# A chunked-scan decay mask built by TensorE in PSUM instead of by broadcast loads, in a hybrid encoder block on one core

## The chip, the cores and the metric

The kernel runs on one core of a Trainium2 chip, in float32. The metric is the device time of one execution in microseconds (us), as the median of several runs; smaller is better.

## The reference

The block takes x (1024 tokens by 1024) and computes h = RMSNorm(x), one combined projection, two mixers side by side, an output projection with a residual, and a squared-ReLU MLP. The first mixer is a Mamba-2 scan that runs over the tokens in both directions, in chunks of 128; the second is neighbourhood attention on q, k and v. What the change touches is the decay matrix inside a chunk of the scan:

```python
a_cum = jnp.cumsum(ac, axis=2)
seg = a_cum[:, :, :, None] - a_cum[:, :, None, :]
decay = jnp.exp(jnp.where(lower, seg, -jnp.inf))
cb = jnp.einsum("bclgn,bcsgn->bclsg", cc, bc)
y_diag = jnp.einsum("bclsge,bcsgep->bclgep", cb[..., None] * decay, xc)
```

For each head there are two such matrices, one for each direction. One fills the upper triangle and the other the lower, so that for one chunk and head both fit in one 128x128 tile: the value at (s, l) is exp(cum(l) - c1(s)), with the forward cum and c1 on one side of the diagonal and the backward ones on the other (c1 is cum less the logarithm of the step dt). Heads are in two groups g of eight, and the chunks c run from 0 to 7.

## The kernel before

Accurate products on TensorE are made of float32r parts: a number is split into a high part (ScalarE, a copy that rounds) and a low part (a subtraction), and `mm3` (lines 177 to 180) issues three matmuls. Weights are split by `load_w` (lines 134 to 152): a load of 512 KB by SyncE into `wraw`, the high part `wh` on ScalarE (L148), the low part `wl` on the engine that the caller names (L149). In the first half of the kernel four buffers hold such pairs; one group of 512 output columns needs all four.

The stages, in the order of the program: RMSNorm and transposes; the projection of x, B and C with their convolution (`xbc`) and the step sizes and decays (`decays`, lines 328 to 424); the gate z (lines 501 to 510); the scan (lines 518 to 680); the projections of q, k and v (`qkv_proj`, lines 684 to 732); attention with the output projection as its filler; the MLP.

**The scan.** Lines 677 to 680 run 16 times `backward(7 - i, g)` and then `forward(i, g)`, for i from 0 to 7 and g in (0, 1). One such pair is called a half-step in what follows. `backward` makes cb = B.C of the chunk on TensorE (`pcb`, L587) and, for the eight heads in two portions q of four, the decay tile: SyncE loads the two cum rows of four heads from DRAM, broadcast to all 128 partitions (`rb`, L605, 512 KB); GpSimd subtracts c1 (two instructions, L612); VectorE puts the backward values below the diagonal (`copy_predicated`, L618); ScalarE takes the exponential (L623); VectorE multiplies with cb (L625); TensorE multiplies with x (`pd`, L630). Then come what earlier chunks carry in (`carried`: `py`, `yo`), the sums into `y1` (GpSimd L638, L641, VectorE L642), and `decay_state` (`xw`, `xh`, `xl`, `pS`, `st`, `sh`, `sl`). `forward` has `carried` and `decay_state` of the other direction. In the last eight half-steps (i from 4 on), both directions of a chunk are complete: `gated` (lines 570 to 579) multiplies with the gate (L574), takes the norm (ScalarE L576, GpSimd L201 and L202, ScalarE L578) and stores the result (L579), and `backward` first fetches what the other direction had stored (`yf`, L648, added by GpSimd in L649).

**The filler.** `qkv_proj` has 6 groups (q, k, v for two halves of the heads) of 8 tiles of 24 matmuls, 1152 in all, named `pq`. A q or k tile is then normed (`normed_split`, lines 693 to 708): ScalarE L695, VectorE L697, GpSimd L201 and L202, VectorE L699, four transposes on TensorE into `ptq` (L705), and the split (L187, L188). This work doesn't depend on the scan.

**What sets the order.** Each engine runs its own list of instructions strictly in order. The lists are made when the program is built: a scheduler (`schedule_with_timeline_sim=True`) takes the instructions by readiness in its own model of the time, and earlier program lines first. PSUM tiles are handed out by tag, in the order of the program's lines: a tile of a tag with two buffers waits until the tile two before it, in that order, has been read for the last time. The tags that matter here: "mm" (3 buffers, `pq`), "s" (2 buffers: `pcb`, `py`, `pS`) and "tp" (2 buffers, `ps_tp`, line 109): in the kernel before, no line of the scan takes a "tp" tile, and `ptq` of the filler does.

Of the kernel before, what the change touches and what calls it, by code (L numbers as in the profile page):

```python
# [9 lines left out]
F32 = mybir.dt.float32  # L10
F32R = mybir.dt.float32r
# [7 lines left out]
P = 128  # L19
# [12 lines left out]
def shape_constants():  # L32
# [5 lines left out]
    cst = np.concatenate([ident, tri_f, tri_b, ones], axis=1)  # L38
# [17 lines left out]
def hymba_block(  # L56
# [58 lines left out]
    def ps_v(name="v"):  # L115
        return phase["ps"].tile([P, 512], F32, tag="v", name=name, bufs=phase["v"])
# [9 lines left out]
    cum_dr = dr.tile([2, P, P], F32, name="cum_dr")  # L126
# [92 lines left out]
    with ExitStack() as ph:  # L219
# [78 lines left out]
        nc.sync.dma_start(cst, cst_d[:, P:].rearrange("p (a f) -> p a f", a=3))  # L298
# [12 lines left out]
        with ExitStack() as p1:  # L311
# [16 lines left out]
            def decays():  # L328
# [189 lines left out]
        with ExitStack() as p2:  # L518
# [14 lines left out]
            st = [[None, None], [None, None]]  # L533

# [46 lines left out]
            def backward(c, g):  # L581
# [18 lines left out]
                pd = ps_v("pd")  # L600
                for q in range(2):
                    h0 = 8 * g + 4 * q
                    rb = qp.tile([P, 2, 4, P], F32, tag="rb", name="rb", bufs=2)
                    r0 = c * 16 + h0
                    nc.sync.dma_start(  # L605
                        rb.rearrange("p d h s -> p d (h s)"),
                        cum_dr[:, r0 : r0 + 4, :]
                        .rearrange("d h s -> d (h s)")
                        .partition_broadcast(P),
                    )  # L610
                    for d in range(2):
                        nc.gpsimd.tensor_tensor(  # L612
                            rb[:, d],
                            rb[:, d],
                            c1[:, d, c, h0 : h0 + 4].unsqueeze(2).broadcast_to([P, 4, P]),
                            op=sub,
                        )
                    nc.vector.copy_predicated(  # L618
                        rb[:, 0],
                        lmask.unsqueeze(1).broadcast_to([P, 4, P]),  # L620
                        rb[:, 1],
                    )
                    nc.scalar.activation(rb[:, 0], rb[:, 0], AF.Exp)  # L623
                    gm = rb[:, 0]
                    nc.vector.tensor_tensor(  # L625
                        gm, rb[:, 0], cb.unsqueeze(1).broadcast_to([P, 4, P]), op=mul
# [768 lines left out]
```

## Time and profile before

| | |
|---|---|
| median of 3 runs (lowest, highest) | 1684.91 us (1677.66, 1690.37) |
| span of the profiled execution, first to last instruction | 1676.4 us |
| TensorE busy | 1590.8 us, 95% |
| VectorE, ScalarE, GpSimd busy | 1106.0, 721.3, 708.4 us |
| scan: first `pcb` read by VectorE, last `pcb` on TensorE | 269.2 us, 581.4 us |
| first matmul of the output projection (`po`) | 672.0 us |

The span is what the profile accounts for; the runs are timed apart from it, and their median is 8.5 us above it. The first 265 us are norm, x, B, C, decays and z. From 265 to 600 us the scan and its filler run together, from 600 to 672 us the rest of the filler alone; then attention to about 1020 us and the MLP to the end. A busy matmul overlaps its neighbours, so counts of matmuls say more than busy time.

### The profile page before, as it was taken

How to read it: one execution, taken by the hardware profiler on the slowest of the kernel's cores; microseconds unless marked ns; L12 is line 12 of the kernel's file. 1: busy time of each engine (PE TensorE's matmuls, PEld its weight loads, DVE VectorE, ACT ScalarE, POOL GpSimd, SP SyncE). 2: the span in 40 equal slices, each digit the busy share in tenths (PEclk: the TensorE clock that was granted, in tenths of full speed). 3: DMA queues.
4: the chain of work that ended last, by engine and by line, in shares of the span. 5: the costliest groups of instructions: out<-in, count | busy, mean ns of one | idle time of the engine just before them, and what ended most of it. 6: DMA issues, size and time to landing. Idle time of an engine off the chain costs nothing. (4 is left out here: it accounts for less than half of the span.)

```text
span 1676.4 us, 20931 instructions
## 1 busy us (share of the span) xinstructions
PE 1590.8 (95%) x7453; PEld 1297.3 (77%) x7453; DVE 1106.0 (66%) x1686; ACT 721.3 (43%) x1187; POOL 708.4 (42%) x506
## 2 busy tenths in 40 slices
PE   6999999998988899998999989999999989999999
PEld 5788888777766678887778767788888868888887
DVE  5767214788796852888898867544243387887863
ACT  5434223434343442556565533554444444433330
POOL 4000003888687862322243232244444465455551
PEclk9999999999999999999999999999999989999999
DMA  8113337876666785956664141353344386644231
GB/s 217 51 38 105 93 100 212 215 194 196 229 220 173 218 263 190 281 165 185 180 190 118 62 164 50 101 201 126 138 164 150 127 295 231 216 149 151 101 101 75
DMA packets 178755, 269.75 MB, mean 161 GB/s; under 512 B 14219, under 2 KB 105307, under 8 KB 178651
## 3 DMA queue, kind: packets, MB, share of 16 engines
q1 hardware_dynamic: 134667, 227.51, 44.1%
q10 hardware_dynamic: 42976, 37.23, 7.3%
q0 software_dynamic: 1008, 3.67, 0.5%
q8 instruction: 59, 0.97, 0.3%
q14 instruction: 45, 0.37, 0.1%
HBM read 185.21 MB, written 86.50 MB: 162 GB/s over the span
## 5 line engine op out<-in xcount | busy, mean ns | idle before, releaser
L760 POOL TENSOR_TENSOR wl<-wraw,wh 128x1024 fp32r<-128x1024 f32 x110 | 298.5, 2724 | 318.4 <-ACT wh L759 297.1
L759 ACT ACTIVATE wh<-wraw 128x1024 fp32r<-128x1024 f32 x110 | 115.6, 1054 | 149.7 <-PE px L745 50.8
L745 PE MATMUL px<-wh,ahl 128*128 128x512 f32 x512 | 162.5, 395 | 3.3 <-ACT ahl L759 3.3
L179 PE MATMUL pq<-wl,hTh 128*128 128x512 f32 x384 | 153.6, 402 | 4.9 <-DVE wl L149 4.8
L178 PE MATMUL pq<-wh,hTh 128*128 128x512 f32 x384 | 154.4, 405 | 3.5 <-ACT wh L148 3.5
L745 PE MATMUL px<-h,wh 128*128 128x512 f32 x496 | 156.0, 396 | 1.4 <-DVE x L1078 1.4
L180 PE MATMUL pq<-wh,hTl 128*128 128x512 f32 x384 | 152.9, 399 | 0.0
L760 DVE TENSOR_TENSOR ahl<-ar,ahl 128x1024 fp32r<-128x1024 f32 x56 | 115.1, 2062 | 23.2 <-ACT ahl L759 22.1
L759 ACT ACTIVATE ahl<-ar 128x1024 fp32r<-128x1024 f32 x56 | 58.2, 1052 | 140.1 <-PE px L745 75.3
L745 PEld LDWEIGHTS px<-wh,ahl 128*128 128x128 f32 x512 | 97.0, 190 | 25.0 <-ACT ahl L759 3.7
L745 PEld LDWEIGHTS px<-h,wh 128*128 128x128 f32 x496 | 93.2, 188 | 24.0 <-ACT h L184 1.6
L149 DVE TENSOR_TENSOR wl<-wraw,wh 128x1024 fp32r<-128x1024 f32 x40 | 55.3, 1386 | 81.9 <-ACT wh L148 81.2
L745 PE MATMUL px<-wl,ahl 128*128 128x512 f32 x256 | 101.0, 395 | 0.0
L745 PE MATMUL px<-h,wl 128*128 128x512 f32 x248 | 98.1, 395 | 0.0
L881 POOL TENSOR_TENSOR mb<-braw,nam 128x256 f32<-128x256 f32 (+1 forms) x48 | 40.1, 863 | 131.1 <-DVE nmx L939 72.2
L179 PEld LDWEIGHTS pq<-wl,hTh 128*128 128x128 f32 x384 | 73.6, 192 | 23.1 <-DVE wl L149 8.6
L149 POOL TENSOR_TENSOR wl<-wraw,wh 128x1024 fp32r<-128x1024 f32 x18 | 43.0, 2401 | 110.5 <-ACT wh L148 110.5
L178 PEld LDWEIGHTS pq<-wh,hTh 128*128 128x128 f32 x384 | 74.0, 193 | 20.2 <-ACT wh L148 5.2
L184 ACT ACTIVATE pth<-ptp 128x384 fp32r<-128x384 f32 (+1 forms) x128 | 57.7, 455 | 73.1 <-PE ptp L962 72.5
L612 POOL TENSOR_TENSOR rb<-rb,c 128x512 f32<-128x512 f32 x64 | 77.0, 1223 | 20.4 <-DMA rb<-cum_dr 19.2
L180 PEld LDWEIGHTS pq<-wh,hTl 128*128 128x128 f32 x384 | 73.5, 191 | 15.0
L745 PE MATMUL pz<-h,wh 128*128 128x512 f32 x256 | 80.8, 396 | 0.8 <-DVE h L185 0.8
(268 smaller groups left out, 4211.4 us busy)
## 6 DMA issues: line engine op xcount, KB each, us to landing
ar<-act_dr SPq DMA_DIRECT2D x56, 512.0 KB, 3.7
act_dr<-cq SPq DMA_DIRECT2D x49, 512.0 KB, 3.2
wraw<-in_w_in_dram SPq DMA_DIRECT2D x44, 512.0 KB, 4.3
rb<-cum_dr SPq DMA_DIRECT2D x32, 512.0 KB, 7.2
wraw<-in_w_mlp_in_dram SPq DMA_DIRECT2D x32, 512.0 KB, 4.6
wraw<-in_w_mlp_out_dram SPq DMA_DIRECT2D x32, 512.0 KB, 5.2
q_dr<-hl ACTq DMA_DIRECT2D x64, 128.0 KB, 3.6
k_dr<-hl ACTq DMA_DIRECT2D x16, 512.0 KB, 5.3
```

The source lines that it names most:

```text
L149: lo_eng.tensor_tensor(lo[:, 0:n], raw[:, 0:n], hi[:, 0:n].bitcast(F32), op=sub)
L178: nc.tensor.matmul(pt, lhsT=ah, rhs=bh, start=first, stop=False)
L179: nc.tensor.matmul(pt, lhsT=ah, rhs=bl, start=False, stop=False)
L180: return nc.tensor.matmul(pt, lhsT=al, rhs=bh, start=False, stop=last)
L184: nc.scalar.activation(hi, src, AF.Copy)
L612: nc.gpsimd.tensor_tensor(rb[:, d], rb[:, d], c1[:, d, c, h0 : h0 + 4].unsqueeze(2).broadcast_to([P, 4, P]), op=sub,)
L745: nc.tensor.matmul(pt, lhsT=a, rhs=b, start=f, stop=l, skip_group_check=True)
L759: nc.scalar.activation(hl[0], src, AF.Copy)
L760: eng.tensor_tensor(hl[1], src, hl[0].bitcast(F32), op=sub)
L881: nc.gpsimd.tensor_tensor(mb[:, s].rearrange("p (s r c) -> p s r c", r=16, c=8), v[:, a:b], nam[:, s].rearrange("p (s r c) -> p s r c", r= ...
```

## The change

The two cum rows are no longer broadcast by a load. `decays` now transposes c1 as well, splits cum and -c1 into high and low parts (float32r), and stores both in DRAM. In the scan the exponent is one matmul of a few rows: the stationary operand `cols` has in rows 0 to 7 the -c1 values of four heads' two directions, high and low, and ones in rows 8 and 9; the moving operand `rows` has indicators in rows 0 to 7, which route the -c1 of each head and direction to its block of 128 columns, and the cum rows (high, low) in rows 8 and 9; all other rows are zero. The result, for two heads and both directions, is a 128x512 tile `seg` in PSUM. `copy_predicated` selects in PSUM, and the exponential reads PSUM. `rows` and `cols` have two buffers each for the whole scan; small loads refresh rows 8 and 9 (`rows`) and 0 to 7 (`cols`). `seg` is taken from the tag "tp".

Two more edits: the low parts of the filler's weights are made by GpSimd and no longer by VectorE, and the scratch for GpSimd's own DMA descriptors is set to 4096 bytes.

```diff
-    cum_dr = dr.tile([2, P, P], F32, name="cum_dr")
+    cum_dr = dr.tile([2, 32, 2, 2, 2, P], F32, name="cum_dr")
+    c1_dr = dr.tile([16, 4, 8, P], F32, name="c1_dr")
...
                     nc.tensor.transpose(ptc[:, d * P : (d + 1) * P], acum[:, d], ident)
-                cum = qp.tile([P, 256], F32, name="cum", bufs=1)
-                nc.vector.tensor_copy(cum, ptc[:, 0:256])
-                for d in range(2):
-                    nc.sync.dma_start(cum_dr[d], cum[:, d * P : (d + 1) * P])
+                    nc.tensor.transpose(ptc[:, (d + 2) * P : (d + 3) * P], c1[:, d], ident)
...
+                split_from_psum(cum[:, 0], cum[:, 1], pv[:, 0])
+                split_from_psum(cm1[:, 0], cm1[:, 1], pv[:, 1], -1.0)
...
+            rows = [qp.tile([P, 2, 512], F32R, name=f"rows{i}", bufs=1) for i in range(2)]
+            cols = [qp.tile([P, 4, P], F32R, name=f"cols{i}", bufs=1) for i in range(2)]
+            for i in range(2):
+                part = qp.tile([P, 512], F32, tag="y1", name="part")
+                nc.sync.dma_start(part, cst_d[:, (4 + 4 * i) * P : (8 + 4 * i) * P])
+                for j in range(2):
+                    if i == 0:
+                        nc.scalar.copy(rows[j][:, 0], part)
+                        nc.scalar.copy(rows[j][:, 1], part)
+                    else:
+                        nc.scalar.copy(cols[j], part.rearrange("p (a s) -> p a s", a=4))
...
+                at = cols[g]
+                nc.sync.dma_start(
+                    at[0:8].bitcast(F32), c1_dr[2 * c + g].rearrange("p r s -> r p s")
+                )
                 for q in range(2):
-                    rb = qp.tile([P, 2, 4, P], F32, tag="rb", name="rb", bufs=2)
-                    nc.sync.dma_start(
-                        rb.rearrange("p d h s -> p d (h s)"),
-                        cum_dr[:, r0 : r0 + 4, :]
-                        .rearrange("d h s -> d (h s)")
-                        .partition_broadcast(P),
-                    )
-                    for d in range(2):
-                        nc.gpsimd.tensor_tensor(
-                            rb[:, d],
-                            rb[:, d],
-                            c1[:, d, c, h0 : h0 + 4].unsqueeze(2).broadcast_to([P, 4, P]),
-                            op=sub,
-                        )
-                    nc.vector.copy_predicated(
-                        rb[:, 0],
-                        lmask.unsqueeze(1).broadcast_to([P, 4, P]),
-                        rb[:, 1],
-                    )
-                    nc.scalar.activation(rb[:, 0], rb[:, 0], AF.Exp)
+                    on = rows[q]
+                    nc.sync.dma_start(
+                        on[8:10].bitcast(F32),
+                        cum_dr[:, 4 * c + 2 * g + q].rearrange("a p h d l -> a p (h d l)"),
+                    )
+                    gm = qp.tile([P, 4, P], F32, tag="gm", name="gm")
+                    for r in range(2):
+                        seg = ps_tp("seg")
+                        nc.tensor.matmul(
+                            seg, lhsT=at[:, 2 * q + r, :], rhs=on[:, r, :], start=True, stop=True
+                        )
+                        both = seg.rearrange("p (h d l) -> p h d l", h=2, d=2)
+                        nc.vector.copy_predicated(
+                            both[:, :, 0], lmask.unsqueeze(1).broadcast_to([P, 2, P]), both[:, :, 1]
+                        )
+                        nc.scalar.activation(gm[:, 2 * r : 2 * r + 2], both[:, :, 0], AF.Exp)
...
-                get = load_w_nat(w_in[0], 0, KD, off + 512 * g, nc.vector)
+                get = load_w_nat(w_in[0], 0, KD, off + 512 * g, nc.gpsimd)
...
-    nc = bacc.Bacc("TRN2", target_bir_lowering=False, num_devices=1)
+    nc = bacc.Bacc(
+        "TRN2", target_bir_lowering=False, num_devices=1, dynamic_dma_scratch_size=4096
+    )
```

The lists of the engines move with it. TensorE in the middle of the scan, around one `pcb` (`pq` is the filler, `py` what earlier chunks carry in); before:

```order
L180 MATMUL pq<-wh,hTl 128x512
L178 MATMUL pq<-wh,hTh 128x512
L587 MATMUL pcb<-cT,bT 128x128
L179 MATMUL pq<-wl,hTh 128x512
L180 MATMUL pq<-wh,hTl 128x512
L178 MATMUL pq<-wh,hTh 128x512
```

and in the change, the first rows of the half-step that begins with this `pcb` (the rest of it are three more `py`, three more `pS` and the four `seg` of a later half-step):

```order
L614 MATMUL pcb<-cT,bT 128x128
L184 MATMUL py<-sh,ch 128x512
L185 MATMUL py<-sl,ch 128x512
L186 MATMUL py<-sh,cl 128x512
L654 MATMUL pd<-xs,gm 128x64 x8
L184 MATMUL pS<-xh,bNh 128x512
L185 MATMUL pS<-xl,bNh 128x512
L186 MATMUL pS<-xh,bNl 128x512
```

Before, 703 of the 1152 `pq` matmuls stand between the third `pcb` and the sixteenth (pq 121 to 824). In the change none does: 120 `pq` stand ahead of the third `pcb`, and the other 1032 stand behind the scan's last matmul.

TensorE at the end of the scan, in the change (`ptq` are the filler's transposes; before, those of most of the 32 q and k tiles stood within the scan):

```order
L641 MATMUL seg<-rows_1907,cols_1909 128x512 x2
L614 MATMUL pcb<-cT,bT 128x128
L185 MATMUL py<-sl,ch 128x512
L186 MATMUL py<-sh,cl 128x512
L729 MATMUL ptq<-ident,qn 128x128 x8
L184 MATMUL py<-sh,ch 128x512
L185 MATMUL py<-sl,ch 128x512
L186 MATMUL py<-sh,cl 128x512
L654 MATMUL pd<-xs,gm 128x64 x8
```

The first `ptq` stands right behind the last `seg`, and the next `pq` behind the last `pd`, so the filler now begins again only there.

GpSimd in the second half of the scan, between two fetches of `yf` (`ry` is the norm's factor, `rb` the decay tile); before:

```order
L649 TENSOR_TENSOR y_2613<-y_2613,yf 128x512
L653 TENSOR_TENSOR xw<-xs,wd 128x512
L612 TENSOR_TENSOR rb<-rb,c_99 128x512 x2
L549 TENSOR_TENSOR st<-st,ed 128x512
L201 TENSOR_SCALAR ry<-ss 128x1
L666 TENSOR_TENSOR y_2666<-y_2666,yo 128x512
L612 TENSOR_TENSOR rb<-rb,c_99 128x512 x2
L202 TENSOR_TENSOR ry<-ry,half 128x1
L672 TENSOR_TENSOR xw<-xs,wd 128x512
```

and in the change:

```order
L673 TENSOR_TENSOR y_2840<-y_2840,yf 128x512
L576 TENSOR_TENSOR st<-st,ed 128x512
L696 TENSOR_TENSOR xw<-xs,wd 128x512
L690 TENSOR_TENSOR y_2893<-y_2893,yo 128x512
L207 TENSOR_SCALAR ry<-ss 128x1
L208 TENSOR_TENSOR ry<-ry,half 128x1
```

The four `rb` instructions around the norm's factor are gone; of the 24 `wl` instructions that GpSimd takes over, 4 stand ahead of the scan's first half-step and 20 behind the last.

More of the change, by code (lines that the diff above doesn't have):

```diff
@@ L37, in shape_constants @@
     ones = np.ones((P, P), np.float32)
-    cst = np.concatenate([ident, tri_f, tri_b, ones], axis=1)
+    rows = np.zeros((2, P, 512), np.float32)
+    for j in range(8):
+        at = 2 * (j // 4) + j % 2
+        rows[0, j, at * P : (at + 1) * P] = 1.0
+    rows[1, 8:10] = 1.0
+    cst = np.concatenate([ident, tri_f, tri_b, ones, *rows], axis=1)
     lmask = (i[None, :] < i[:, None]).astype(np.int32)
@@ L297, in hymba_block @@
         cst = sp.tile([P, 3, P], F32, name="cst")
-        nc.sync.dma_start(cst, cst_d[:, P:].rearrange("p (a f) -> p a f", a=3))
+        nc.sync.dma_start(cst, cst_d[:, P : 4 * P].rearrange("p (a f) -> p a f", a=3))
         tri_f, tri_b, ones = (cst[:, i] for i in range(3))
@@ L420, in decays @@
                     nc.tensor.transpose(ptc[:, d * P : (d + 1) * P], acum[:, d], ident)
-                cum = qp.tile([P, 256], F32, name="cum", bufs=1)
-                nc.vector.tensor_copy(cum, ptc[:, 0:256])
-                for d in range(2):
-                    nc.sync.dma_start(cum_dr[d], cum[:, d * P : (d + 1) * P])
+                    nc.tensor.transpose(ptc[:, (d + 2) * P : (d + 3) * P], c1[:, d], ident)
+                pv = ptc.rearrange("p (x d l) -> p x d l", x=2, d=2)
+                cum = qp.tile([P, 2, 2, P], F32R, tag="dg", name="cum", bufs=1)
+                cm1 = qp.tile([P, 2, 2, P], F32R, tag="zs", name="cm1")
+                split_from_psum(cum[:, 0], cum[:, 1], pv[:, 0])
+                split_from_psum(cm1[:, 0], cm1[:, 1], pv[:, 1], -1.0)
+                for i in range(2):
+                    nc.sync.dma_start(
+                        cum_dr[i].rearrange("m p h d l -> (m p h) d l"), cum[:, i].bitcast(F32)
+                    )
+                nc.sync.dma_start(
+                    c1_dr.rearrange("m p (h r) s -> (m p h) r s", r=4),
+                    cm1.bitcast(F32).rearrange("p a d s -> p (a d) s"),
+                )
             def xbc(fts):
@@ L533, in hymba_block @@
             st = [[None, None], [None, None]]
+            rows = [qp.tile([P, 2, 512], F32R, name=f"rows{i}", bufs=1) for i in range(2)]
+            cols = [qp.tile([P, 4, P], F32R, name=f"cols{i}", bufs=1) for i in range(2)]
+            for i in range(2):
+                part = qp.tile([P, 512], F32, tag="y1", name="part")
[6 more added lines that the diff above has]
+                        nc.scalar.copy(cols[j], part.rearrange("p (a s) -> p a s", a=4))
             def decay_state(d, c, g, xw):
@@ L625, in backward @@
                     nc.vector.tensor_tensor(
-                        gm, rb[:, 0], cb.unsqueeze(1).broadcast_to([P, 4, P]), op=mul
+                        gm, gm, cb.unsqueeze(1).broadcast_to([P, 4, P]), op=mul
                     )
```

4 lines of the change are left out of this document (1 added, 3 removed).

## The prediction

> **What bounds the kernel now.** The page's parts 1 and 2 come first: busy time, and its course over 40 slices.
>
> ```profile
> PE 1590.8 (95%) x7453; PEld 1297.3 (77%) x7453; DVE 1106.0 (66%) x1686; ACT 721.3 (43%) x1187; POOL 708.4 (42%) x506
> PE   6999999998988899998999989999999989999999
> ```
>
> TensorE is the bound of nearly every slice; slices 7 to 14 of 40, the scan, are the dent. So time is TensorE's work plus its idle time. The windows give it for the opening and, in its last four rows, the stage the change touches: start of the scan, its two halves, the filler's rest (PE is the first busy column, DVE the third, POOL the fifth; then the granted clock).
>
> ```profile
> 0.00:42.00 42.00, 28.32 (x130) 23.18 (x131) 22.21 (x27) 22.71 (x37) 18.23 (x19) 0.96 0.90 217
> 265.00:305.00 40.00, 37.14 (x178) 30.59 (x177) 23.46 (x39) 14.18 (x23) 25.67 (x24) 0.96 0.93 281
> 305.00:451.00 146.00, 135.54 (x661) 109.72 (x661) 125.09 (x185) 55.53 (x98) 116.70 (x103) 0.99 0.74 205
> 451.00:600.00 149.00, 129.55 (x602) 100.81 (x601) 116.82 (x164) 64.16 (x120) 118.13 (x115) 0.97 0.68 201
> 600.00:672.00 72.00, 69.66 (x320) 57.12 (x318) 25.30 (x34) 21.86 (x33) 25.70 (x27) 0.98 0.73 231
> ```
>
> In the 295 us from 305 to 600, TensorE idles only 10.5 + 19.5 = 30 us, VectorE and GpSimd are busy about 80%: the scan is slow, but the filler keeps TensorE fed. How slow, VectorE's reading of `pcb` shows, once a half-step:
>
> ```profile
> 306.13 0.29 DVE L593 SCALAR_TENSOR_TENSOR pcb<-pcb,ident 128x128 f32<-128x128 f32 x1
> 430.89 0.28 DVE L593 SCALAR_TENSOR_TENSOR pcb<-pcb,ident 128x128 f32<-128x128 f32 x1
> 586.16 0.29 DVE L593 SCALAR_TENSOR_TENSOR pcb<-pcb,ident 128x128 f32<-128x128 f32 x1
> ```
>
> These are the third, ninth and sixteenth: 124.8 / 6 = 20.8 us a half-step in the first half, 155.3 / 7 = 22.2 in the second. The same windows for `pq` alone:
>
> ```profile
> 265.00:305.00 40.00, 30.14 (x121) 22.66 (x119) 2.98 (x4) 3.13 (x5) 0.96 0.93 281
> 305.00:451.00 146.00, 99.05 (x391) 72.26 (x392) 11.94 (x16) 10.36 (x16) 0.99 0.74 205
> 451.00:600.00 149.00, 96.41 (x367) 69.39 (x365) 11.15 (x15) 10.71 (x16) 0.97 0.68 201
> ```
>
> Of 1152 filler matmuls about 760 run inside the two halves. At the pitch of the timeline, 305.87 - 305.64 = 0.23 us (0.2285 over longer stretches), that is 173 us of work that costs the scan nothing.
>
> ```profile
> 304.06 1.00 PE L630 MATMUL pd<-xs,rb 128*128 128x64 f32 x8
> 304.90 0.44 PE L587 MATMUL pcb<-cT,bT 128*128 128x128 f32 x2
> 305.64 0.39 PE L179 MATMUL pq<-wl,hTh 128*128 128x512 f32 x1
> 305.87 0.39 PE L180 MATMUL pq<-wh,hTl 128*128 128x512 f32 x1
> ```
>
> **The change, part by part.** *The filler leaves the scan.* `seg` takes the PSUM tag "tp", which until now only the filler's `ptq` used here. Tags are handed out in program order, and all 64 `seg` precede all filler lines: no `ptq` can run before the last `seg` is read. Two q tiles get as far as their norm (two `qn` buffers), three more fill the "mm" buffers, and 5 x 24 = 120 matmuls on the filler stops. The lists say just this: 120 `pq` ahead of the third `pcb`, the next behind the last `pd`. TensorE runs its list in order, so what was a mixed stage becomes scan, then filler. Its length is worked out from the third `pcb` (304.9 us before).
>
> *Start.* The first `seg` needs `cols`, whose `part` load stands on SyncE's queue behind the sixteen loads of the bias table:
>
> ```profile
> 273.35 11.67 SPq L529 DMA_DIRECT2D t_dr<-t_dr  x16
> 277.93 0.75 DVE L618 COPY_PREDICATED rb<-lmask,rb 128x512 f32<-128x512 int32 x1 [0.93 <-POOL rb L612]
> t_dr<-t_dr SPq DMA_DIRECT2D x16, 192.0 KB, 4.8
> ```
>
> 285 us, about 5 to land, two copies on ScalarE (1.3), a small load (3): the first `seg` at 295 us, 17 us behind the first `copy_predicated` of before. From there the third `pcb` took 27 us (304.9 - 277.9); two half-steps at the pace below, partly overlapped, take about 18: third `pcb` at 313, bounds 305 (all won back) and 322 (nothing).
>
> *First half of the scan, six half-steps.* What VectorE does per half-step is a floor. Its groups from 262 to 610 us:
>
> ```profile
> L618 DVE COPY_PREDICATED rb<-lmask,rb 128x512 f32<-128x512 int32 x32 | 41.3, 1292 | 16.3 <-POOL rb L612 16.1
> L541 DVE TENSOR_TENSOR xl<-xw,xh 128x512 fp32r<-128x512 f32 x28 | 24.8, 886 | 7.8 <-ACT xh L540 7.7
> L554 DVE TENSOR_TENSOR sl<-st,sh 128x512 fp32r<-128x512 f32 x28 | 23.8, 850 | 0.2
> L625 DVE TENSOR_TENSOR rb<-rb,pcb 128x512 f32<-128x512 f32 x32 | 21.2, 678 | 4.3 <-ACT rb L623 4.2
> L567 DVE TENSOR_TENSOR yo<-py,e 128x512 f32<-128x512 f32 x28 | 19.0, 679 | 1.2 <-POOL y L641 1.2
> L550 DVE TENSOR_TENSOR st<-st,pS 128x512 f32<-128x512 f32 x24 | 16.2, 674 | 0.0
> L574 DVE TENSOR_TENSOR y<-y,sz 128x512 f32<-128x512 f32 x16 | 15.9, 994 | 8.6 <-POOL y L649 6.0 <-POOL y L666 2.6
> L563 DVE TENSOR_TENSOR cl<-cT,ch 128x128 fp32r<-128x128 f32 x28 | 11.8, 424 | 0.0
> L642 DVE TENSOR_TENSOR y<-y,pd 128x512 f32<-128x512 f32 x16 | 10.9, 679 | 12.9 <-POOL y L641 12.9
> L597 DVE SCALAR_TENSOR_TENSOR cf<-dt,cd,dsk 128x8 f32<-128x8 f32 x16 | 7.1, 444 | 0.3
> ```
>
> With 9.5 us of smaller ones, the sum less L618 is 160 us. No row shows `copy_predicated` in PSUM on 256 values: bounds are half of the 0.75 us above (0.37) and all of it, I take 0.45 (x64 = 29 us). 189 / 16 = 11.8 us. L541, L554 and L574 have the shape of the rows at 0.68 us and are longer, so they wait for something while GpSimd works; at 0.68 they save 5.8 + 4.8 + 5.0 = 16 us, and with `copy_predicated` at 0.37 the floor is (160 - 16 + 24) / 16 = 10.5. TensorE's own work is 12 x 0.23 + 4 `seg` x 0.23 + two `pd` portions (2.0) + `pcb`: 6 us, under it. I take 12, bounds 10.5 and 15 (a fifth of waits on top): 313 + 72 = 385.
>
> *Second half, eight half-steps.* Here a chain through `y1` (two buffers) decides: gate, square, norm, scale, store, and only then may GpSimd write the next `y1`, whose `yf` must be fetched before the next gate. One turn of before:
>
> ```profile
> 441.69 1.52 DVE L574 TENSOR_TENSOR y<-y,sz 128x512 f32<-128x512 f32 x1 [3.12 <-POOL y L649]
> 446.79 0.53 POOL L201 TENSOR_SCALAR ry<-ss 128x1 f32<-128x1 f32 x1
> 448.64 2.94 POOL L612 TENSOR_TENSOR rb<-rb,c 128x512 f32<-128x512 f32 x2
> 451.54 0.55 POOL L202 TENSOR_TENSOR ry<-ry,half 128x1 f32<-128x1 f32 x1
> 453.79 0.33 ACTq L579 DMA_DIRECT2D y_dr<-y  x1
> 456.82 1.23 POOL L638 TENSOR_TENSOR y<-xs,cf 128x512 f32<-128x512 f32 x1 [2.47 <-DMA y_dr<-y]
> 462.55 1.28 POOL L649 TENSOR_TENSOR y<-y,yf 128x512 f32<-128x512 f32 x1 [2.14 <-DMA yf<-y_dr]
> 463.86 1.52 DVE L574 TENSOR_TENSOR y<-y,sz 128x512 f32<-128x512 f32 x1 [1.66 <-POOL y L649]
> ```
>
> 22.2 us. The four L612 on it (2.1 + 2.9 = 5.1 us) go, the gate falls from 1.52 to about 0.7; the store and the fetch stay: 22.2 - 5.1 - 0.8 = 16.3, I take 16.5, bounds 13 (VectorE's load and one transfer) and 20.5. The last half-steps update no state: less 8. Last `pd` at 385 + 132 - 8 = 509 us (before 600).
>
> *Filler alone.* 1032 x 0.2285 = 236 us, 30 tiles' four `ptq` at 0.15 us each (18), and the 3 us of attention that lie before 672 now: 257, say 255 as some `ptq` run in the scan's tail. The weights' low parts on GpSimd: 20 of 24 fall here. A group's last tile frees a pair every 6 x 0.23 = 1.4 us, GpSimd needs 2.4 for each:
>
> ```profile
> L149 POOL TENSOR_TENSOR wl<-wraw,wh 128x1024 fp32r<-128x1024 f32 x2 | 4.7, 2390 | 25.7 <-ACT wh L148 25.7
> ```
>
> With ScalarE's high part ahead (about 1.1 us, also serial), the fourth pair is ready about 2.5 us late: 5 boundaries, 12 us, bounds 0 (other instructions hide it) and 25 (the norm's power between them). VectorE, freed of them, is not the bound in this stretch.
>
> *At nothing:* the extra transposes and splits in `decays` (under x-projection matmuls, where slices are full), the freed 512 KB broadcasts, the descriptor scratch (7 loads at GpSimd's queue; up to a few us each if hidden no longer).
>
> **Sum.** 509 + 255 + 12 = 776 us against 672: +104 us. Against the profiled span 1676.4 that is 1780; its median of runs lies 8.5 above, so 1684.9 + 104 = **1789 us**, slower. A measurement of this kernel tells 1% from no change.
>
> **Rivals.** *The second half keeps its pace.* Store and fetch are untouched, and in-order waits may refill what L612 leaves: 21 us a turn instead of 16.5 gives +36, 1825. For it: two DMA waits, 2.47 and 2.14, in the turn above; against it: L612 stands bodily between the norm's two instructions.
>
> *A lower TensorE clock.* In the scan TensorE is busy half the time. The first window above, 67% busy, still had 0.96, which speaks against. At half clock 6 us of work become 12, as much as a half-step: about +3 on six and +1 on eight, 26 us, 1815. The Trainium skill, "TensorE: Matmul & The Clock Gate" (Part 1: The HAM clock gate), says the clock halves after an idle window of about 3.4 us; by that rule the fetch of `yf`, with TensorE waiting, would do it, and no row here shows such a gap without filler.
>
> *Not slower.* The scan alone becomes so short that scan plus filler fits into the old stage. The point: last `pd` by 672 - 267 = 405 us, (405 - 313 + 8) / 14 = 7.1 us a half-step; at 6.5 it would be 1677. For it: GpSimd loses 64 L612 and the scan's VectorE loses all filler work. Against it: VectorE's floor of 10.5.
>
> **How the numbers follow.** Forecast 0.67; slow second half 0.15; clock 0.13; not slower 0.05 (faster 0.03, within 1% 0.02). Low end: third `pcb` at 305, half-steps of 11 and 13.5, no boundary stall: 305 + 66 + 108 - 8 + 255 = 726, +54, 1739. High end: 316, half-steps of 15 and 18.5, stalls of 20: 316 + 90 + 148 - 8 + 275 = 821, +149, 1834; the clock and the slow second half each lie inside, both together do not (1851), so I set 1845.
>
> **What would show it.** In the profile after: no `pq` between about 300 and 500 us, TensorE near half busy there, half-steps of 12 and then 16.5 us, `pq` without a gap from about 509 to 776 us but for waits on GpSimd's `wl` at five places, `po` first at about 776. It is wrong if `pq` runs among the `seg`, if half-steps come under 10 us, or if the granted clock of the scan's windows falls well below 0.9.

## The result, and the profile after

The changed kernel takes 1760.36 us (median of 4 runs, 1758.5 to 1768.66) beside 1683.89 us for the kernel before (4 runs, 1677.66 to 1690.37). The ratio is 1.0478, with a 95% interval of 1.0446 to 1.0511: slower by 4.8%, some 76 us. The span of the profiled execution is 1756.8 us, before 1676.4.

Part 1 of the page after, and the course of TensorE's busy time and of its granted clock over the 40 slices:

```profile
PE 1647.4 (94%) x7519; PEld 1340.6 (76%) x7519; DVE 1064.6 (61%) x1695; ACT 736.6 (42%) x1227; POOL 674.5 (38%) x466
PE   6999999766799999999999999899999999999999
PEclk9999999886699999999999999899999999999999
```

There is now one deep dent, in slices 7 to 10 (the first is slice 0), and the clock has the same dent. TensorE's busy time went up by 57 us. `seg` is a part of it; matmuls that are "busy" longer at a lower clock are another, so that lost time is counted as work. The windows after, cut where the stages now end (start of the scan, first half, second half, filler alone; columns as before):

```profile
265.00:305.00 40.00, 38.00 (x174) 30.33 (x173) 17.65 (x32) 15.38 (x29) 20.15 (x17) 1.00 0.64 205
305.00:375.00 70.00, 54.48 (x220) 40.68 (x220) 61.74 (x126) 28.27 (x66) 41.45 (x38) 0.83 0.32 105
375.00:484.00 109.00, 76.72 (x259) 57.13 (x259) 89.08 (x159) 48.16 (x109) 70.44 (x77) 0.66 0.41 127
484.00:744.00 260.00, 253.84 (x1171) 209.03 (x1172) 78.07 (x111) 77.57 (x110) 117.70 (x98) 0.99 0.55 164
```

In the 179 us from 305 to 484 TensorE runs 479 matmuls; before, 661 + 602 stood in 295 us. VectorE is busy 150.8 of the 179 us. The same stretches for the filler's `pq` alone:

```profile
265.00:305.00 40.00, 28.35 (x120) 22.46 (x120) 1.50 (x2) 1.38 (x2) 1.00 0.64 205
305.00:484.00 179.00, 0.00 (x0) 0.00 (x0) 0.00 (x0) 1.38 (x2) 0.73 0.37 119
484.00:744.00 260.00, 244.38 (x1032) 192.25 (x1032) 33.73 (x45) 30.20 (x44) 0.99 0.55 164
```

120, then none in the whole scan, then 1032: the two stages stand one behind the other. The pace of the scan, by VectorE's reading of the third, ninth and sixteenth `pcb`, as before:

```profile
307.60 0.29 DVE L620 SCALAR_TENSOR_TENSOR pcb<-pcb,ident 128x128 f32<-128x128 f32 x1
375.45 0.28 DVE L620 SCALAR_TENSOR_TENSOR pcb<-pcb,ident 128x128 f32<-128x128 f32 x1
476.15 0.30 DVE L620 SCALAR_TENSOR_TENSOR pcb<-pcb,ident 128x128 f32<-128x128 f32 x1
```

67.9 / 6 = 11.3 us a half-step in the first half and 100.7 / 7 = 14.4 in the second; before 20.8 and 22.2. So the scan by itself did become faster, and the kernel slower: first `po` at 743.7 us instead of 671.9, which is 72 of the 80 us between the spans. The other 8 us passed later. The profiled execution of the kernel before is its fastest of the four (1677.66 us), so a part of such a difference can be the spread between executions.

### The profile page after: what moved, and what is told of

Read it like the earlier page. It is cut to its first block, busy times and chain, and to the rows that moved or that the text cites. A ratio compares the mean times of both kernels' runs of the same rounds, so it can differ in the third digit from the quotient of the medians.

```text
span 1756.8 us, 21115 instructions
## 1 busy us (share of the span) xinstructions
PE 1647.4 (94%) x7519; PEld 1340.6 (76%) x7519; DVE 1064.6 (61%) x1695; ACT 736.6 (42%) x1227; POOL 674.5 (38%) x466
## 5 line engine op out<-in xcount | busy, mean ns | idle before, releaser
L784 POOL TENSOR_TENSOR wl<-wraw,wh 128x1024 fp32r<-128x1024 f32 x110 | 298.1, 2721 | 319.7 <-ACT wh L783 307.6
L155 POOL TENSOR_TENSOR wl<-wraw,wh 128x1024 fp32r<-128x1024 f32 x42 | 102.1, 2448 | 251.1 <-ACT wh L154 248.1
L783 ACT ACTIVATE wh<-wraw 128x1024 fp32r<-128x1024 f32 x110 | 115.8, 1056 | 150.0 <-PE px L769 52.0
L185 PE MATMUL pq<-wl,hTh 128*128 128x512 f32 x384 | 150.8, 393 | 0.7 <-POOL wl L155 0.7
L154 ACT ACTIVATE wh<-wraw 128x1024 fp32r<-128x1024 f32 x58 | 61.1, 1060 | 62.0 <-DMA wraw<-in_w_in_dram 19.7
L185 PEld LDWEIGHTS pq<-wl,hTh 128*128 128x128 f32 x384 | 72.5, 189 | 15.6 <-POOL wl L155 1.0
L973 ACT ACTIVATE pr<-pr,nmx 128x384 f32<-128x384 f32 (+1 forms) x128 | 75.0, 587 | 17.2 <-DVE nmx L963 16.3
```

The costliest lines, as they stand in the source:

```text
L154: nc.scalar.activation(hi[:, 0:n], raw[:, 0:n], AF.Copy)
L155: lo_eng.tensor_tensor(lo[:, 0:n], raw[:, 0:n], hi[:, 0:n].bitcast(F32), op=sub)
L185: nc.tensor.matmul(pt, lhsT=ah, rhs=bl, start=False, stop=False)
L783: nc.scalar.activation(hl[0], src, AF.Copy)
L784: eng.tensor_tensor(hl[1], src, hl[0].bitcast(F32), op=sub)
L973: nc.scalar.activation(pr[:, 0:n], pr[:, 0:n], AF.Exp, bias=nmx[:, b : b + 1], scale=-1.0, accum_out=db,)
```

## The experiments

One theory stood at the start, with its rivals. *A: the tag.* `seg` shares "tp" with the filler's `ptq`, and that alone keeps the filler out. *Rivals:* the scan's new chain is itself the cost (B in the first expectations), or GpSimd's split of the filler's weights (C there), or the low clock. When the first runs had left 1% unexplained, the question became what holds the versions that untie the tag above the kernel before: GpSimd (now called B), the number of banks (now C), or the order in which the list puts scan and filler (F to H). One kernel before ran beside each group: 1679.3 us for the first four, 1683.6 for the next four, then 1681.8, 1681.2 and 1680.8.

### A bank of its own for `seg`

```diff
-        enter_phase(ph, 1, 3, 1)
+        enter_phase(ph, 1, 2, 1)
...
-                        seg = ps_tp("seg")
+                        seg = phase["ps"].tile([P, 512], F32, tag="sg", name="seg", bufs=1)
```

(With "v" kept at one bank, so that the bank comes from the filler's "mm".)

> The change with seg taken from a PSUM bank of its own (one buffer; the matmul tag gets two instead of three), all else as in the change. Theory A (the shared tag keeps the filler out of the scan): the filler runs between the scan's matmuls again, granted clock of the scan above 0.95, first matmul of the output projection back from 744 to 665 to 680 us, total 1670 to 1695. Rival B (the new chain itself, its reads of PSUM and its thin matmuls, makes the scan stage longer): the total stays above 1740. Rival C (GpSimd with the weights' low parts is the brake): above 1720, with TensorE waiting for wl inside the scan.

Measured: 1698.21 us, ratio 1.0104 (1.0077 to 1.0132), first `po` at 683.9. Its `pq` from 305 us on:

```profile
305.00:480.00 175.00, 127.36 (x502) 93.07 (x503) 15.69 (x21) 14.37 (x21) 0.99 0.48 146
480.00:672.00 192.00, 132.11 (x508) 97.28 (x506) 15.70 (x21) 14.31 (x21) 0.96 0.65 191
```

502 filler matmuls run where the change had none, and of 4.8% of loss 1.0% is left: nearly four fifths go with the tag. Time and `po` lie 3 and 4 us above what A had expected; this version also takes a bank from the filler, and what that costs is measured below.

### The tag alone, in the kernel before

```diff
-                pcb = ps_s("pcb")
+                pcb = ps_tp("pcb")
```

> The kernel before with one word changed: pcb of the scan is taken from the tag tp, so no seg, no GpSimd weights. Theory A: the filler stops after 120 matmuls here too; the old, slower chain then runs alone at 15 to 19 us a half-step, output projection from about 770 to 810 us, total 1780 to 1820. Rivals B and C: nothing that they blame is in this kernel, so it stays within 1% of before, 1670 to 1700.

Measured: 1806.39 us, ratio 1.0765 (1.074 to 1.079), first `po` at 799.6. Its `pq` in the scan:

```profile
305.00:480.00 175.00, 0.00 (x0) 0.00 (x0) 0.00 (x0) 0.00 (x0) 0.56 0.49 138
```

With nothing changed but one tag, the filler is out and 127 us are lost. Theory A holds in both directions. The new arithmetic is a gain by comparison: with the filler out in both, the scan from the fourth to the sixteenth `pcb` takes 200 us here (308.0 to 508.2) and 158 in the change (317.9 to 475.5).

### GpSimd's split of the weights, undone and done alone

```diff
-                get = load_w_nat(w_in[0], 0, KD, off + 512 * g, nc.gpsimd)
+                get = load_w_nat(w_in[0], 0, KD, off + 512 * g, nc.vector)
```

> The change with the filler's low parts on VectorE as before. Theory A: 1750 to 1770, no difference beyond 0.7%, since TensorE waited only 0.7 us for wl on GpSimd. Rival C: most of the 76 us come back, below 1710.

> The kernel before with only the filler's low parts moved to GpSimd. Theory A: the filler stays within the scan, total within 1% of before (1670 to 1700), perhaps a few us slower since GpSimd is busy 80% in the scan and each of 20 pieces takes 2.4 us. Rival C: 1730 or more.

Measured: in the change, back on VectorE, 1748.29 us, ratio 1.0426 (1.0388 to 1.0463), against 1.0478 (1.0446 to 1.0511): 8 to 12 us better, first `po` 7 us earlier, though the two intervals still overlap. In the kernel before, on GpSimd, 1693.34 us, ratio 1.0086 (1.0069 to 1.0103), first `po` 11.6 us later; there TensorE waits 14.6 us in `ptq<-qn` behind the norm that GpSimd also makes. In the kernel before this is a second and smaller cost. That it explains the rest of the version above was tempting, and is tried next.

### Both mends together, and the bank by itself

The version with a bank of its own, its weights on VectorE:

> The change with `seg` in a bank of its own (taken from the filler's three) and with the filler's weights split on VectorE again, so that of the change only the scan's new arithmetic is left. The same with the split on GpSimd stood 1.0% above the kernel before, and the split on GpSimd alone, put into the kernel before, cost 0.9%. Theory B, that all of that rest is GpSimd's split: 0.3% below to 0.4% above the kernel before (1674 to 1687 us beside 1679), first `po` at 670 to 676 us instead of 683.9. Theory C, that the rest is the third bank that the filler gave up, or the scan's new chain of PSUM reads: at least 0.7% above (1691 to 1699 us), first `po` at 680 or later.

And the kernel before, with one of its three "mm" banks left unused:

> The kernel before with one bank of the filler's three left unused, and nothing else. Theory B: the filler's third bank is worth little, 0.3% or less (1675 to 1684 us beside 1679), since while the scan runs it is TensorE that is full, and behind it there is one group of 24 matmuls in work and one being read out. Theory C: the bank is worth 0.6 to 1.2% (1689 to 1700 us), with waits of `pq` on the reader of its bank, 10 us or more in the first 672 us.

Measured: both mends 1712.45 us, 1.0182 (1.0165 to 1.02); the kernel before with two banks 1723.6 us, 1.0243 (1.0222 to 1.0265), first `po` at 710.8. Theory B falls: VectorE's split makes the mended version slower, not faster. Theory C is the nearer one, and the cost is larger than I had put it: the bank is worth 2.4%. TensorE in the first 265 us of the kernel before, with three banks and with two:

```profile
0.00:265.00 265.00, 251.32 (x1160) 206.35 (x1161) 134.00 (x151) 102.58 (x133) 20.45 (x41) 0.99 0.37 98
```

```profile
0.00:265.00 265.00, 245.49 (x1120) 200.45 (x1121) 130.24 (x148) 98.98 (x128) 22.15 (x41) 0.99 0.36 96
```

40 matmuls fewer (9 us at 0.23): `px` and `pz` of the earlier stages take "mm" too. Every version with two banks loses about this much there, ahead of the scan. The rest comes later: from 265 us to the first `po` TensorE idles 52 us instead of 35, and its granted clock is 0.92 instead of 0.97. With two banks less filler stands between the scan's steps in the list (763 matmuls ahead of the last `pcb` instead of 824), and the waits for their inputs come to the surface (the longest of TensorE from 265 us on, with two banks; waited for, us in total, times, longest):

```profile
PE pd L630 <- DVE rb L625: 12.9, 9, 4.3
PE ptq L705 <- DVE qn L699: 9.8, 5, 4.9
PE pd L630 <- DVE y L642: 8.2, 1, 8.2
```

The Trainium skill, "Perfetto Trace Analysis" (Optimizing Tensor Performance, Matmuls), says that independent groups of matmuls should rotate through PSUM banks so that one is read out while the next is computed. The third bank's 2.4% fits that, but theory C's sign, waits of `pq` on the reader of its bank, is not among the longest waits, so the trace doesn't show that this is how the bank earns its time. With two banks on both sides the change is the faster one: 1698.2 beside 1723.6 us with its split on GpSimd, and 1712.5 with the split on VectorE as in the kernel before.

### `ptq` in the filler's own banks

```diff
-                tp = ps_tp("ptq")
+                tp = ps_mm("ptq")
```

> The change with the filler's `ptq` taking its bank from the filler's own three (`mm`) instead of the two of `tp` that `seg` goes round in. Theory A, that the tag which filler and scan share is what keeps the filler out: filler matmuls now run between the third and the last `pcb`, but only as many as three banks for `pq` and `ptq` together let through, perhaps a fifth to a half of the 1032 that stood behind the scan, so the time comes between the two, 1705 to 1745 us, with the first `po` at 695 to 735. Rival: the filler stays out because the scan's chain fills TensorE's queue in program order; then no `pq` runs in 305 to 480 us, and the time stays at 1750 to 1765.

Measured: 1873.24 us, ratio 1.1138 (1.1105 to 1.117), the slowest of all; first `po` at 854.8. 216 filler matmuls ran from 305 to 480 us, as A says, and yet both expected times were missed. Handed out in program order, a `ptq` that waits for its norm now holds a bank ahead of later `pq`. Between one group of 24 and the next, in the stretch behind the scan (start, duration, and in brackets the wait):

```profile
609.87 1.09 PE L729 MATMUL ptq<-ident,qn 128*128 128x128 f32 x4 [4.40 <-DVE qn L723]
610.61 0.78 PE L184 MATMUL pq<-wh,hTh 128*128 128x512 f32 x1
611.19 0.63 PE L185 MATMUL pq<-wl,hTh 128*128 128x512 f32 x1
611.61 0.63 PE L186 MATMUL pq<-wh,hTl 128*128 128x512 f32 x1
615.58 0.39 PE L184 MATMUL pq<-wh,hTh 128*128 128x512 f32 x1
```

(Rows are left out between 611.61 and 615.58.) Group and norm alternate, with 4.4 us of nothing, and behind each gap the matmuls come every 0.43 us instead of 0.23 for about 5 us: 13 us a group instead of 5.5.

### Is it the clock?

```diff
+                for _ in range(3):
+                    nc.tensor.matmul(
+                        pcb[:, 2 * P :], lhsT=bT[:, g, cs], rhs=cT[:, g, 0 : 2 * P],
+                        start=True, stop=True,
+                    )
                 cb = pcb[:, 0:P]
```

(and the same three behind the first portion's `pd`; nothing reads them.)

> The change with six more matmuls (128x128 by 128x256, fp32) in each of the 16 backward half-steps, three behind `pcb` and three behind the first four of `pd`, into the unused half of `pcb`'s bank; nothing reads them. They are 0.55 us each at the full clock, by the 275 ns of `pcb` at 128 columns, so 3.3 us per half-step. In the change the granted clock fell to 0.80 and 0.64 in the stretch where only the scan runs, and `pd` took 3.67 us instead of 2.00. Theory D, that the low clock sets the scan's pace there: with TensorE fuller the granted clock of 305 to 480 us rises to 0.9 or more, `pd` goes back to about 2 us, and the last `pcb` comes earlier than the 475.5 us of the change, at 455 to 472 us, with the first `po` 5 to 20 us earlier. Theory E, that the pace is set by VectorE's and ScalarE's links and the low clock lies beside them: the last `pcb` comes 5 to 50 us later (up to 3.3 us per half-step where the matmuls stand in the way), whatever the clock does.

Measured: 1780.47 us, ratio 1.0585 (1.0563 to 1.0607), last `pcb` at 489.9 us, first `po` at 760.7. Its windows:

```profile
305.00:400.00 95.00, 78.56 (x367) 60.51 (x366) 80.28 (x160) 34.06 (x81) 54.43 (x47) 0.93 0.29 95
400.00:480.00 80.00, 59.31 (x229) 43.82 (x230) 56.38 (x106) 32.08 (x77) 52.66 (x56) 0.80 0.40 124
```

The clock rose from 0.80 and 0.64 in the same windows of the change to 0.93 and 0.80, and the scan ended 14 us later. This is nearer to E, but not clean: the added matmuls (96, each two passes) stand in TensorE's list ahead of `seg` and `pd`, so a gain from the clock may be hidden under their own 192 passes, which come 0.22 us apart at the full clock, 42 us in all. What bounds the clock's cost is VectorE in the change's trace. It is busy 84% of the scan and waits for TensorE mainly here, from 305 to 484 us:

```profile
DVE st L577 <- PE pS L186: 15.7, 8, 3.2
DVE seg L645 <- PE seg L641: 2.1, 1, 2.1
```

With two more of 0.5 us each that is 19 us of 179. All idle time of VectorE there is 28 us, the waits for ScalarE and GpSimd included. As far as VectorE sets the pace, TensorE's slowness cost no more than these 28 us; how much of them a full clock would have saved isn't shown.

### Three banks for the filler, and the tag untied

Here `seg` goes to the scan's own pair of banks, and ScalarE copies `pcb`'s 128 columns out so that its bank comes free (the scratch `jk` leaves the bank too):

```diff
-                cb = pcb[:, 0:P]
-                jk = pcb[:, P : 2 * P]
+                cb = qp.tile([P, P], F32, name="cb", bufs=2)
+                nc.scalar.copy(cb, pcb[:, 0:P])
+                jk = qp.tile([P, P], F32, name="jk", bufs=1)
...
-                        seg = ps_tp("seg")
+                        seg = ps_s("seg")
```

> The change with `seg` in the scan's own two banks (tag `s`, with `pcb`, `py` and `pS`), `tp` left to the filler and the filler's three banks kept; so that `pcb`'s bank comes free, ScalarE copies its 128 columns to SBUF and the readers take them there. Measured so far: a bank of the filler's three is worth 2.4% to the kernel before, and with two banks for the filler in both the change stood 25 us below the kernel before (1698 beside 1724). Theory F, that the scan's new arithmetic is a gain and the whole loss is one of banks: filler matmuls run through the scan (200 or more in 305 to 400 us), first `po` at 640 to 668 us, and the time is 1650 to 1676, 0.5 to 2% below the kernel before. Rival G, that `seg`, `pcb`, `py` and `pS` in one pair of banks make a half-step wait for its own readers: the filler runs on, but the scan ends later than in the kernel before (last `pcb` after 625 us instead of 581.6), attention waits for `y`, first `po` at 680 or later, and the time is 1690 or more.

> The same with the filler's weights split on VectorE. With two banks for the filler the split on VectorE was the slower one (1712 beside 1698), on the kernel before and on the change as it is the faster one (by 14 and 12 us). Theory F with the split being a cost where VectorE is full and the filler runs beside the scan: 5 to 18 us above the same kernel with the split on GpSimd, VectorE busier in 305 to 600 us. Rival: GpSimd's split is a cost of itself (2.4 us for one, before which the filler waits), then this one is 5 to 15 us below.

Measured: 1699.0 us, 1.0097 (1.0081 to 1.0114), and with VectorE's split 1703.36 us, 1.0129 (1.0115 to 1.0143). Theory F falls on the time; the numbers are those of G, last `pcb` at 650.3, first `po` at 686.6. VectorE's split is the slower one here by 4 us, just under the 5 to 18 expected. To tell whether crowded banks were the reason, the two banks of "tp" were made two tags, one for `seg` and one for `ptq`, with nothing added:

```diff
-        return ps.tile([P, 512], F32, tag="tp", name=name, bufs=2)
+        if bank is None:
+            bank = phase["t"] = 1 - phase.get("t", 1)
+        return ps.tile([P, 512], F32, tag=f"tp{bank}", name=name, bufs=1)
...
-                        seg = ps_tp("seg")
+                        seg = ps_tp("seg", 0)
...
-                tp = ps_tp("ptq")
+                tp = ps_tp("ptq", 1)
```

> The change with the two banks of `tp` made two tags of one bank: `seg` always takes the one, `ptq` always the other, every other user of `tp` takes them in turn. So scan and filler no longer share a tag, the filler keeps its three banks, and no copy is added; `seg` has one bank (as where it had a bank of its own, 1698 us) and `ptq` one instead of two. Theory A and C (the shared tag is the loss of the change, the third bank the rest): filler matmuls run through the scan, and the time falls to 1660 to 1700 us. Within that: if what now sets the end is that the filler, with three banks, runs ahead of the scan and leaves its end uncovered (as with `seg` in the scan's banks, last `pcb` 650.3, first `po` 686.6 us), the last `pcb` comes after 630 us, the first `po` at 680 to 692, and the time is 1690 to 1705; if it was the scan's crowded banks there, the last `pcb` comes by 615 us and the first `po` at 650 to 675, with 1660 to 1685 us. If neither bank nor tag but the new arithmetic holds the filler, 1740 or more.

Measured: 1696.63 us, 1.0086 (1.0058 to 1.0114), last `pcb` at 636.2, first `po` at 683.9: the branch in which the filler runs ahead. TensorE from 600 us on, in the kernel before and then here:

```profile
600.00:672.00 72.00, 69.66 (x320) 57.12 (x318) 25.30 (x34) 21.86 (x33) 25.70 (x27) 0.98 0.73 231
```

```profile
600.00:672.00 72.00, 44.62 (x200) 35.21 (x198) 37.11 (x66) 26.25 (x56) 33.79 (x35) 0.78 0.75 244
```

Up to 600 us this is the best version: TensorE idles only 5 us from 265 to 600, where the kernel before idles 33. Then it gives all of it back. The filler's last matmul starts at 632 us, the scan still runs, and nothing is left to lie beside its end. Two waits of attention follow, on k and on the scan's y:

```profile
PE psc L957 <- DMA k<-k_dr: 19.5, 1, 19.5
PE pty L833 <- DMA yl<-y_dr: 6.1, 1, 6.1
```

k itself had long been computed (its stores run from 344 us on). Its load stands in SyncE's list behind the scan's last load (`y<-y_dr`). The kernel before, and this one:

```profile
600.68 0.32 SPq L665 DMA_DIRECT2D y<-y_dr  x1
603.26 1.28 SPq L855 DMA_DIRECT2D k<-k_dr  x2
```

```profile
657.56 0.38 SPq L691 DMA_DIRECT2D y<-y_dr  x1
658.74 1.51 SPq L881 DMA_DIRECT2D k<-k_dr  x2
```

The place in the list is only a part of the wait. From the issue at 658.74 to `psc` at 673.8 another 15 us pass, in which the 16 DMA engines are full (share 1.03 from 655 to 674 us): ten loads of x, 256 KB each, and one of q, 1024 KB, stand shortly ahead of k's in SyncE's list.

### Less filler ahead of the scan's end

The last version turns this round: `seg` in two banks, `ptq` in one, `pq` in two ("v" again kept at one bank; the diff is against the version just above).

```diff
-        enter_phase(ph, 1, 3, 1)
+        enter_phase(ph, 1, 2, 1)
...
-                        seg = ps_tp("seg", 0)
+                        nseg = phase["q"] = phase.get("q", 0) + 1
+                        seg = ps_tp("seg", 0) if nseg % 2 else phase["ps"].tile(
+                            [P, 512], F32, tag="sg", name="seg", bufs=1
+                        )
```

> The version before this one (`seg` and `ptq` in tags of their own), with the third bank of the filler given to `seg`: two banks for `seg`, one for `ptq`, two for `pq`. In the built lists the filler matmuls that stand ahead of the sixteenth `pcb` are 824 of 1152 in the kernel before, 120 in the change, 932 with `seg` in a bank of its own, 1152 with the tags apart (where the filler ran out at 641 us, the scan went on alone to 650 and attention waited 26 us for k and y) and 740 here. Theory H, that with the tag untied the time is set by how far the list lets the filler run ahead, since the filler is the only cover of the scan's end: here 412 filler matmuls (94 us) are left for the end, no wait of attention on k or y above 2 us, the last `pcb` at 530 to 585 us (13 half-steps of about 17 us from 307, with TensorE full, up to 21), first `po` at 640 to 675, and the time is 1655 to 1688, the best of all versions and level with or below the kernel before. Rival C, that the filler's third bank is worth its 2.4% here too, whatever the order: waits of `pq` and `ptq` on their readers, first `po` at 695 or later, 1705 to 1730 us.

Measured (the filler ran out at 632 us in the version before, not at 641): 1715.24 us, 1.0204 (1.0169 to 1.0238), last `pcb` at 578.5, first `po` at 707.7. Theory H is right on the order and wrong on the time: the scan ended as early as in the kernel before and attention waited 1.3 us on k and not at all on y, but the time is rival C's. Its longest wait of TensorE from 265 us on:

```profile
PE ptq L732 <- DVE qn L726: 13.6, 8, 5.3
```

The versions that bear on banks and order, in one table ("ahead" is the number of the 1152 filler matmuls that stand ahead of the sixteenth `pcb` in TensorE's built list; a `pcb` is two passes, and the table has the start of the second):

| version | banks of `pq` | split on | ahead | last `pcb`, us | first `po`, us | ratio |
|---|---|---|---|---|---|---|
| before | 3 | VectorE | 824 | 581.6 | 671.9 | 1 |
| the change | 3 | GpSimd | 120 | 475.7 | 743.7 | 1.0478 |
| before, two banks | 2 | VectorE | 763 | 591.3 | 710.8 | 1.0243 |
| `seg` in a bank of its own | 2 | GpSimd | 932 | 615.5 | 683.9 | 1.0104 |
| the same | 2 | VectorE | 1138 | 649.8 | 699.9 | 1.0182 |
| `seg` in the scan's banks | 3 | GpSimd | 1152 | 650.3 | 686.6 | 1.0097 |
| the same | 3 | VectorE | 1152 | 656.7 | 693.5 | 1.0129 |
| `seg` and `ptq` apart | 3 | GpSimd | 1152 | 636.2 | 683.9 | 1.0086 |
| two banks for `seg` | 2 | GpSimd | 740 | 578.5 | 707.7 | 1.0204 |

Two things go against each other in the versions with the tag untied. With three banks for the filler, the lists put all of it ahead of the scan's end. With two banks some of it is left for the end (little with VectorE's split: 14 matmuls), but the first 265 us lose 9 us and TensorE waits more on the way: from 265 to 600 us it idles 19 and 27 us in the two with GpSimd's split, instead of 5. No version tried beats the kernel before.

## Why the prediction was right, point by point

**The mechanism held.** The forecast was that the shared tag shuts the filler out of the scan, and the stages add up. The trace shows 0 `pq` in the scan, and the experiments on the tag show it as the cause: the tag alone brings the loss into the kernel before, and two tags in place of one take most of it out of the change. Slower, as forecast; the size was 76 us where the sum had 104, inside the range.

**Start.** The first `seg` ran at 295 us, as worked out; the third `pcb` came at 306.8, the forecast was 313. Nearly all of the late start was won back, which was the low bound.

**First half: 12 us a half-step forecast, 11.1 measured** (306.8 to 373.3 on TensorE). VectorE was the floor, as argued; its groups from 262 to 500 us, those to set beside the rows of before:

```profile
L568 DVE TENSOR_TENSOR xl<-xw,xh 128x512 fp32r<-128x512 f32 x28 | 25.5, 911 | 10.0 <-ACT xh L567 10.0
L645 DVE COPY_PREDICATED seg<-lmask,seg 128x256 f32<-128x256 int32 x64 | 25.5, 422 | 2.1 <-PE seg L641 2.1
L581 DVE TENSOR_TENSOR sl<-st,sh 128x512 fp32r<-128x512 f32 x28 | 23.0, 820 | 0.0
L601 DVE TENSOR_TENSOR y<-y,sz 128x512 f32<-128x512 f32 x16 | 14.9, 933 | 2.2 <-POOL y L690 1.4 <-POOL y L673 0.9
```

`copy_predicated` in PSUM took 0.42 us, where 0.45 was taken from bounds of 0.37 and 0.75. The rows that I had put at 0.68 for the low bound, without GpSimd's subtractions, stayed long (0.91, 0.82 and 0.93). GpSimd was still busy 111.9 of the 179 us; whether that is the reason isn't shown.

**Second half: 16.5 forecast, 15.6 measured** (373.3 to 466.7, six half-steps), and the last `pd` at 483 instead of 509. One turn of the chain through `y1`, as before:

```profile
436.45 1.52 DVE L601 TENSOR_TENSOR y<-y,sz 128x512 f32<-128x512 f32 x1
446.11 1.28 POOL L665 TENSOR_TENSOR y<-y,yo 128x512 f32<-128x512 f32 x1
450.76 1.26 POOL L673 TENSOR_TENSOR y<-y,yf 128x512 f32<-128x512 f32 x1 [1.70 <-DVE st L577]
452.83 1.41 DVE L601 TENSOR_TENSOR y<-y,sz 128x512 f32<-128x512 f32 x1
```

16.4 us from gate to gate, with this gate still at 1.5 us; the turn's other gate, at 441.25, took 0.68. GpSimd's add of `yf` waits here for VectorE and not for the fetch. Of the six adds in this half, three wait for VectorE (6.4 us in all) and two for the fetch (2.6 us); before, three of six waited for the fetch (6.1 us). So the chain of store and fetch, which the first rival made the bound, still held up two turns, and lay beside VectorE's list in the others.

**Filler alone: 255 us forecast; 258 measured** (first `pq` behind the scan at 486.1, first `po` at 743.7). **Boundary stalls: 12 forecast, 0.7 measured.** This is the term that was mis-sized by its mechanism. TensorE's waits from 484 to 744 us:

```profile
PE ptq L729 <- DVE qn L723: 5.1, 3, 2.1
PE pq L185 <- POOL wl L155: 0.7, 1, 0.7
```

I reckoned that a pair of weights is turned over every 6 matmuls, 1.4 us, where GpSimd needs 2.4. The built list weaves the first two tiles of a group, so that a pair serves 12 matmuls, 2.7 us, and GpSimd keeps up: in the group that begins at 557 us the first uses of its four pairs, at 557.7, 560.4, 563.1 and 565.9, each come behind the end of their split. With the split back on VectorE the change was 8 to 12 us faster, but 6.0 of the 7 us at `po` are already there at the last `pcb` (475.7 against 469.7 us), in the scan, where GpSimd makes no `wl`. So how the split would cost them stays open.

**Sum:** `po` at 744 instead of 776; of these 32 us, 26 are the scan's (the start 6, the first half 6, the second 14) and 11 the stalls, less 5 of small ones between. Behind `po` another 8 us passed that no step foresaw. In the profiles of the other versions it is between 2 and 13 us, against the same execution of the kernel before, its fastest; the cause stays open.

**The clock.** Here I argued wrongly, and a sign that I had named for a wrong prediction came true. From a window that was 67% busy at 0.96 I took it that the clock would stay; it fell to 0.83 and 0.66. Two portions' `pd` of eight each at the full and at the low clock:

```profile
355.43 2.00 PE L654 MATMUL pd<-xs,gm 128*128 128x64 f32 x16 [0.71 <-DVE gm L649]
408.42 3.68 PE L654 MATMUL pd<-xs,gm 128*128 128x64 f32 x16 [0.52 <-DVE gm L649]
```

The rule of the Trainium skill, "TensorE: Matmul & The Clock Gate" (Part 1: The HAM clock gate), is that the clock halves after an idle window of about 3.4 us. Some of the traces agree. In the version with `ptq` in "mm" the clock is 0.50 from 608.4 to 615.2 us, at the end of a gap of 4.4 us. Even the window that I argued from has a stretch at 0.50, from 20.7 to 24.1 us, at the end of a wait of 3.66 us. The first half of the change's scan doesn't agree: there the clock fell three times, at 321, 342 and 365 us, and no wait of TensorE was longer than 1.62 us. Of the last of the three, first the longest wait ahead of it (in brackets), then the windows before and behind the fall (the granted clock is the third number from the end):

```profile
363.99 0.50 PE L184 MATMUL py<-sh,ch 128*128 128x512 f32 x1 [1.62 <-DVE st L577]
362.10:365.50 3.40, 1.24 (x6) 0.56 (x4) 3.40 (x10) 1.37 (x3) 1.54 (x3) 1.00 0.21 80
365.50:372.30 6.80, 6.43 (x23) 5.85 (x24) 4.43 (x8) 1.73 (x5) 4.51 (x4) 0.50 0.37 115
```

In the 3.4 us ahead of the three falls TensorE was busy about 1.4, 1.7 and 1.2 us: several short waits close together were enough here, and the measurement decides. The step that failed is that the busy share of a window of 42 us was read as if its idle time were spread evenly. The low clock also hid itself: I expected TensorE near half busy in the scan, and it shows 73% (131.2 of 179 us), since a slow matmul is busy longer. But the rival's price, 26 us on top of the sum, didn't come: at the low clock both halves were still shorter than the sum had them, TensorE's longer instructions lay mostly beside VectorE's 84%, and VectorE's direct waits for TensorE sum to 19 us.

**Not slower:** the mended versions show how much room there was. Where both sides have two banks the whole change is worth 25 us (1.4% by the ratios), and the change without GpSimd's split, so that both sides split on VectorE, 11 us (0.6%). With `seg` and `ptq` apart it saves 28 us of TensorE's idle time from 265 to 600 us. But `seg` adds 64 x 0.23 = 15 us to the engine that is 95% busy, and the kernel before had idle time of only 35 us from 265 us to `po` to win.

## What to carry to other kernels

A PSUM tag is a queue in program order: when an early stage takes tiles from a tag that its filler uses too, the filler gets none of them before the stage's last tile and comes to a stop, however idle the engine is (here after 120 of 1152 matmuls). So look for shared tags before counting instructions. When a stage that has filler beside it becomes faster, see who ends last: the filler is worth most beside the end of the scan, and one that runs out before the scan does leaves the loads that stand behind the scan in SyncE's list uncovered, as k's 19.5 us showed. Untying a tag with a bank from the filler has a price of its own: the bank was worth 2.4% to the kernel before, half of what the whole change lost. And a busy share over a long window says little about the clock; look at stretches of a few us.

## What the runs showed of the hardware

After a gap of 4.4 us TensorE's 128x512 matmuls came every 0.43 us instead of 0.23 for about 5 us; in a scan with no filler the granted clock was 0.56 over 175 us (the kernel before with `pcb` in "tp"), 0.73 over 179 us in the change. In the first half of that scan it fell to 0.50 three times, with no wait of TensorE over 1.62 us. A multiply on VectorE became slower when its operand moved from PSUM to SBUF, beside GpSimd at work, from 265 to 690 us; `seg` and `ptq` apart, then `seg` in the scan's banks with the copy:

```profile
L651 DVE TENSOR_TENSOR gm<-gm,pcb 128x512 f32<-128x512 f32 x32 | 21.8, 681 | 5.5 <-ACT gm L650 5.4
```

```profile
L650 DVE TENSOR_TENSOR gm<-gm,cb 128x512 f32<-128x512 f32 x32 | 32.5, 1017 | 11.8 <-ACT gm L649 11.6
```

1.02 us instead of 0.68 for the same shape; why, no run settles. VectorE spent 11 us more on this multiply in the version with the copy, beside ScalarE's own time. What stays open is a version that keeps three banks for the filler and holds part of it back until the scan's end; it wasn't tried.
